# A branch for each weight tile instead of each pair of tiles, in a mixture-of-experts stage on TensorE

## The chip, the cores and the metric

The kernel runs on one core of one Trainium2 chip. The metric is device time in microseconds, from launch to end, as the median of the runs shown. TensorE (PE) multiplies, VectorE (DVE) and ScalarE (ACT) work on elements, SyncE (SP) issues the loads from HBM.

## The reference, cut to what matters

A two-layer backbone for 256 tokens of width 1024. The part that the change touches is the last one, a top-2-of-8 mixture of SwiGLU experts with an inner width of 3584, all in float32:

```python
def moe_swiglu(h, router_w, wg, wu, wd):
    logits = (h @ router_w).astype(jnp.float32)
    top_v, top_i = lax.top_k(logits, TOP_K)
    gates = jax.nn.softmax(top_v, axis=-1)
    dense_gate = jnp.sum(jax.nn.one_hot(top_i, N_EXPERTS, dtype=jnp.float32)
                         * gates[..., None], axis=-2).astype(h.dtype)
    out = jnp.zeros_like(h)
    for e in range(N_EXPERTS):
        out = out + dense_gate[..., e:e + 1] * swiglu(h, wg[e], wu[e], wd[e])
    return out
```

where `swiglu(h, wg, wu, wd)` is `(silu(h @ wg) * (h @ wu)) @ wd`.

## The kernel before, in words

Each expert's tokens are gathered by a product with a one-hot matrix (`Expert.gather`, L1103) into at most 128 columns, and after the expert scattered back in the same manner (`scatter`, L1178). The expert's weights come in tiles of 128 x 2048 float32, 1 MB each, in the order in which they are used (`Weights`, L908): 336 tiles for the eight experts, 42 for one expert. A tile is loaded by SP into one of six raw buffers (L934), then split into two float32r parts: ACT casts it to the high part `mh` (L948), and DVE subtracts that from the tile for the low part `ml` (L949). Either part has five buffers, so a split can run at most some tiles ahead of the products that read it.

The inner width is cut into seven chunks of 512 (`NCH`). A chunk has two tiles of the gate matrix (group G), two of the up matrix (group U) and, one chunk later, two of the down matrix (group D). G and U go into a PSUM bank each, are copied by ACT (`copied`, L1136), turned by PE (`turn`, L1141: transposes, or products with `fold`), go through the SiLU on ACT and the product on DVE (`act`, L1150, tile `m_sg`), and are split again into `moe_aT`, the stationary operand of D.

An expert with fewer than 65 tokens is **light**: its activations' high and low parts stand side by side in one stationary operand of 128 columns, so that two products for each weight slice (L1078, L1079) do what takes three (L142 to L144) in a **full** expert. Which it is, is known only at run time, so PE holds both versions and chooses with a branch (`arms`, L1189, branch at L1194). Expert 0 has no branch (`lights[0]` is None) and is always full.

`group` (L1213) writes out one group of two tiles. Before its products it has the splits of two later tiles written out, and between these two the work that was kept in `late`: what follows the group before (copies, SiLU, `moe_aT`, the gating of an expert's result) and the gathers and scatters that `after` has put on a later step. Then come the two tiles' products inside one branch. With `tiles.stop` the first tile behind the group, the lines are

```python
for n in range(tiles.stop + 1, tiles.stop + 4):
    W.split(n)
    W.load(n + 6)
    if n == tiles.stop + 2:
        while late:
            late.pop(0)()
parts = [W.parts.pop(n) for n in tiles]
arms(light, lambda arm: body(parts, arm))
```

A split with argument n has all tiles below n split. In the order of the source, a group's products therefore stand behind the splits of three tiles beyond the group. The order in which ACT, DVE and SP finally work is not this one: the framework's scheduler places each instruction by its own account of when it could run. A branch's two bodies are one unit to it, into which nothing else is put; what belongs to other engines lies in the stretch between two branches.

Of the kernel before, what the change touches and what calls it, by code (L numbers as in the profile page):

```python
# [18 lines left out]
P = 128  # L19
D = 1024  # L20
KT = D // P
# [7 lines left out]
D_FE = 3584  # L29
# [45 lines left out]
def hybrid_kernel(  # L75
# [26 lines left out]
    def bank(name, pool=None):  # L102
        pool = pool or psa
        return pool.tile([P, 512], F32, tag="bank", name=name)
# [518 lines left out]
    for s, (k0, k1) in enumerate(STAGES):  # L623
# [8 lines left out]
        w = split(qk, f"qk{k0}")  # L632
        modulated(hT, rx, m_x, hm, k0, k1, "xx")

        def products(rows, which, f0):
            for i in which:
                for k in range(k0, k1):
                    rows.one(i, k, *(p(k - k0)[:, f0:f0 + 512] for p in w))
                if k1 == KT:
                    rows.done(i, rows.pss[i])  # L640
# [267 lines left out]
    class Weights:  # L908
# [17 lines left out]
        @staticmethod  # L926
        def down(e, ci):
            return [(moe_w_down[e, 2 * ci + b], 2) for b in range(2)]
# [24 lines left out]
    W = Weights()  # L953
# [96 lines left out]
    def pick(w, e, *at):  # L1050
        return w[(e, *at)] if isinstance(e, int) else w[(bass.ds(e, 1), *at)].rearrange("o p f -> (o p) f")
# [31 lines left out]
    def whole(src, k, name):  # L1083
        return split(load(src, k, name), name, True)

    class Expert:
# [40 lines left out]
            self.ohT = sp.tile([P, S], F32R, tag="ohT", name=self.n + "_ohT")  # L1127
            A.copy(self.ohT, self.po[:, :S])

        def up(self, o, parts, light):  # L1130
            for half in range(2):
                for j in range(4):
                    k = 4 * half + j
                    products(o, self.xg, k, tuple(w[:, j, :] for w in parts[half]), light, k == 0, k == KT - 1)

        def copied(self, o, name):  # L1136
            c = x2k(name)
# [3 lines left out]
        def turn(self, pts, gu, light):  # L1141
            for pt, src in zip(pts, gu):
                for i in range(4):
                    o = pt[:, i * P:(i + 1) * P]
                    if light:
                        T.matmul(o, src[:, i * P:(i + 1) * P], fold, start=True, stop=True)
                    else:
                        T.transpose(o, src[:, i * P:(i + 1) * P], ident)
# [5 lines left out]
            self.aT = in_pairs(at[:, 1024 * (ci % 2):1024 * (ci % 2) + 1024], 4)  # L1154
            split_pairs(self.aT, sg)

        def down(self, ci, parts, light):
            aT = self.aT
            for b in range(2):
                k0 = ci * 4 + 2 * b  # L1160
                last = k0 + 2 == D_FE // P
                for j, i in [(j, i) for i in range(2) for j in range(2)] if last else [(j, i) for j in range(2) for i in range(2)]:
                    o = slice(i * 512, (i + 1) * 512)
                    products(self.y[i], aT, 2 * b + j, tuple(w[:, j, o] for w in parts[b]), light, k0 + j == 0, k0 + j == D_FE // P - 1)

        def down_half(self, i, parts, light):

            for k in range(4):
                products(self.y[i], self.aT, k, tuple(w[:, k, :] for w in parts[0]), light, False, k == 3)

        def gated(self, i):
            src = x2k(f"{self.n}_yg{i}")
# [16 lines left out]
    def arms(light, body):  # L1189

        if light is None:
            body(False)
        else:
            with tc.If(light > 0) as narrow:  # L1194
                body(True)
            with narrow.Else():
                body(False)

    ex = Expert(0, posm, 0, "m0")
# [5 lines left out]
    lights = [None] * NE  # L1205
# [5 lines left out]
    late = []  # L1211

    def group(light, body, then=lambda: None):  # L1213

        nonlocal step
        tiles = W.groups[step]
        for n in range(tiles.stop + 1, tiles.stop + 4):
            W.split(n)
            W.load(n + 6)
            if n == tiles.stop + 2:  # L1220
                while late:
                    late.pop(0)()
        parts = [W.parts.pop(n) for n in tiles]
        arms(light, lambda arm: body(parts, arm))
        late.append(then)
        late.extend(todo_after.pop(step, ()))
        step += 1

    def turned(x, ci, gu):
        pts = [bank(f"{x.n}_{ci}_t{m}", psb) for m in range(2)]  # L1230
        return pts, (lambda arm: x.turn(pts, gu, arm)), (lambda: x.act(ci, pts))
# [3 lines left out]
    for e in range(NE):  # L1235
        light = lights[e]
        for ci in range(NCH):
            gu = []
            _, turn, acted = turned(ex, ci - 1, prev[2]) if ci else nothing
            if ci:  # L1240
                behind.clear()
            o = bank(f"{ex.n}_{ci}_0")
            places = ci == 0
            if places:
                ex.po = bank(ex.n + "_ohp", psb)

            def gates_up(parts, arm, o=o):
                turn(arm)
                if places:
                    ex.places(arm)  # L1250
                ex.up(o, parts, arm)

            def gates_then(o=o, ex=ex, ci=ci, gu=gu, acted=acted, places=places):
                if places:
                    ex.placed()
                acted()
                gu.append(ex.copied(o, f"{ex.n}_{ci}_g"))

            group(light, gates_up, gates_then)
            u = bank(f"{ex.n}_{ci}_1")  # L1260
            group(light, lambda parts, arm: ex.up(u, parts, arm), lambda u=u, x=ex, ci=ci, gu=gu: gu.append(x.copied(u, f"{x.n}_{ci}_u")))
            if (e, ci) == (0, 1):
                over = gates()
                flush()
            if prev is not None:
                px, pi, _ = prev
                if pi == 0:
                    px.y = [bank(f"{px.n}_y{i}", psc) for i in range(2)]
                if ci == NCH - 1:
                    _, turn, acted = turned(ex, ci, gu)  # L1270
                else:
                    turn, acted = nothing[1:]

                def downs(parts, arm):
                    px.down(pi, parts, arm)
                    turn(arm)

                def downs_then(acted=acted, px=px, pi=pi):
                    acted()
                    if pi == NCH - 1:  # L1280
                        ys = [px.gated(i) for i in range(2)]
                        for i in range(2):
                            for t in range(NT):
                                after(1 + 2 * i + t, lambda x=px, t=t, i=i: x.scatter(t, i, ys[i], first=x.e == 0))

                group(lights[px.e], downs, downs_then)
            if ci == NCH - 3 and e + 1 < NE:
                nxt = Expert(e + 1, posm, (e + 1) % 2, f"m{e + 1}")
                nxt.positions()
                for b in range(2):  # L1290
                    after(b, lambda b=b, x=nxt: x.gather(b))
            prev = (ex, ci, gu)
        last = ex
        if e + 1 < NE:
            ex = nxt
            lights[e + 1] = nc.values_load(few[0:1, e + 1:e + 2], engines=(mybir.EngineType.PE,), min_val=0, max_val=1)
    for i in range(2):
        group(lights[-1], lambda parts, arm: last.down_half(i, parts, arm))
        y = last.gated(i)
        for t in range(NT):  # L1300
            last.scatter(t, i, y, pool=psb)
            store(t, i)


    with tc.If(over > 0):
        pos2 = sp.tile([P, NT, NE], F32, tag="pos2", name="pos2")
        V.tensor_scalar(pos2, posm, -float(P), None, op0=ALU.add)
        with tc.For_i(0, NE) as ev:
            ex = Expert(ev, pos2, 0, "v")
            ex.positions()  # L1310
            for b in range(2):
                ex.gather(b)
            ex.po = bank("v_ohp", psb)
            ex.places(False)
            ex.placed()
            ex.y = [bank(f"v_y{i}", psc) for i in range(2)]

            for ci in range(NCH):
                gu = []
                for m in range(2):  # L1320
                    o = bank(f"v_{ci}_{m}")
                    ex.up(o, [whole(pick((moe_w_gate, moe_w_up)[m], ev, ci, half), 4, f"v{ci}_{m}_w{half}") for half in range(2)], False)
                    gu.append(ex.copied(o, f"v_{ci}_{m}c"))
                _, turn, acted = turned(ex, ci, gu)
                turn(False)
                acted()
                ex.down(ci, [whole(pick(moe_w_down, ev, 2 * ci + b), 2, f"v{ci}d{b}") for b in range(2)], False)
            for i in range(2):
                y = ex.gated(i)
                for t in range(NT):  # L1330
                    ex.scatter(t, i, y)
        for i in range(2):
            for t in range(NT):
                store(t, i)
# [52 lines left out]
```

## Time and profile before

| | us |
|---|---|
| median of 3 runs (1473.71 to 1480.41) | 1473.93 |
| the profiled execution, its own time | 1478.5 |
| its span, from the first to the last instruction | 1476.7 |
| granted clock of TensorE over the span, 1 is full | 0.987 |

The eight experts run from about 506 us to the end; in order they are full, light, light, light, full, full, light, light, and each but the first begins at the transposes of line 1124. In a row of a timeline stand the start, the duration, the engine, the line, the operation and `out<-in`, and in brackets how long the engine stood idle before it and what ended that. A matmul's duration is longer than its share of the engine, since matmuls overlap: the step from one start to the next is what it costs.

### The profile page before, as it was taken

The numbers are of one execution on the slowest core, as the hardware profiler recorded it, in microseconds if no ns is written. First come the engines' busy times: TensorE is split into PE (matmuls) and PEld (weight loads), VectorE is DVE, ScalarE is ACT, GpSimd is POOL, SyncE is SP. The second block draws the span as 40 slices with busy tenths as digits, with TensorE's granted clock in tenths as the row PEclk, the third lists the DMA queues.
The fourth block names the chain that finished last, engine by engine and source line by source line (L and its number), as shares of the span: only waits on it lengthen the run. The fifth ranks groups of instructions, "written<-read, shape, count | busy, mean of one in ns | idle before, by whom it ended". The sixth has DMA issues, their size and how long they took to land.

```text
span 1476.7 us, 19854 instructions
## 1 busy us (share of the span) xinstructions
PE 1390.9 (94%) x7746; PEld 1151.7 (78%) x7746; DVE 1226.8 (83%) x1256; ACT 974.0 (66%) x891; POOL 1.9 (0%) x7
## 2 busy tenths in 40 slices
PE   6999999999999999999989989999999999899897
PEld 4667789999979888877767767777888888677675
DVE  4687588776666698899999998998888879899897
ACT  3444354433354576788887887886777768788785
POOL 0000000000000000000000000000000000000000
PEclk9999999999999999999999999999999999999999
DMA  9554488776654698899998998998978988899894
GB/s 367 226 219 166 155 335 323 286 274 251 245 224 176 240 402 330 326 340 395 403 398 343 408 398 334 416 385 338 365 294 331 365 343 349 331 421 386 336 413 189
DMA packets 66784, 473.53 MB, mean 321 GB/s; under 512 B 7376, under 2 KB 7760, under 8 KB 9696
## 3 DMA queue, kind: packets, MB, share of 16 engines
q1 hardware_dynamic: 66464, 471.16, 82.0%
q8 instruction: 93, 1.52, 0.4%
q0 software_dynamic: 192, 0.56, 0.2%
q14 instruction: 35, 0.29, 0.1%
HBM read 470.64 MB, written 1.05 MB: 319 GB/s over the span
## 4 chain that ended last, share of the span: by engine, by line
PE 59%; DVE 20%; issue 9%; ACT 8%; DMA 5%; DVEq 0%; SPq 0%; ACTq 0%
DVE ml L949 13%; ACT mh L948 5%; PE m L142 5%; PE m L144 5%; PE m L143 5%; PE fg_ps L164 4%; PE fd L164 4%; PE fu_ps L164 4%; PE m_y L144 2%; PE m_y L142 2%; PE m_y L143 2%; PE so_ps L164 2%; PE ada L259 2%; PE su_ps L164 2%; DMA mw<-in_moe_w_gate_dram 1%
## 5 line engine op out<-in xcount | busy, mean ns | idle before, releaser
L949 DVE TENSOR_TENSOR ml<-mw,mh 128x2048 fp32r<-128x2048 f32 x336 | 757.1, 2286 | 47.9 <-ACT mh L948 44.9
L948 ACT CAST mh<-mw 128x2048 fp32r<-128x2048 f32 x336 | 631.2, 1910 | 12.4 <-PE so_ps L164 4.1
L1079 PE MATMUL m<-ml,m_xg 128*128 128x512 f32 x560 | 223.3, 399 | 5.7 <-DVE ml L949 5.7
L1078 PE MATMUL m<-mh,m_xg 128*128 128x512 f32 x560 | 224.1, 400 | 0.0
L1078 PE MATMUL m_y<-mh,moe_aT 128*128 128x512 f32 x280 | 118.2, 422 | 25.3 <-DVE moe_aT L218 21.4
L142 PE MATMUL m<-mh,m_xg 128*128 128x512 f32 x336 | 134.5, 401 | 0.6 <-ACT m_xg L217 0.6
L1079 PE MATMUL m_y<-ml,moe_aT 128*128 128x512 f32 x280 | 121.3, 433 | 13.8 <-DVE ml L949 11.9
L1079 PEld LDWEIGHTS m<-ml,m_xg 128*128 128x128 f32 x560 | 105.2, 188 | 37.0 <-DVE ml L949 14.6
L144 PE MATMUL m<-mh,m_xg 128*128 128x512 f32 x336 | 132.9, 396 | 0.0
L143 PE MATMUL m<-ml,m_xg 128*128 128x512 f32 x336 | 132.7, 395 | 0.0
L1078 PEld LDWEIGHTS m<-mh,m_xg 128*128 128x128 f32 x560 | 105.3, 188 | 22.6
L1079 PEld LDWEIGHTS m_y<-ml,moe_aT 128*128 128x128 f32 x280 | 56.4, 201 | 45.3 <-DVE ml L949 34.3
L1078 PEld LDWEIGHTS m_y<-mh,moe_aT 128*128 128x128 f32 x280 | 56.7, 203 | 41.3 <-ACT mh L948 19.3
L217 ACT CAST moe_aT<-m_sg 128x512 fp32r<-128x512 f32 x56 | 37.4, 669 | 72.5 <-DVE m_sg L1153 72.5
L142 PEld LDWEIGHTS m<-mh,m_xg 128*128 128x128 f32 x336 | 65.6, 195 | 13.3 <-ACT m_xg L217 1.5
L144 PEld LDWEIGHTS m<-mh,m_xg 128*128 128x128 f32 x336 | 65.5, 195 | 12.5
L143 PEld LDWEIGHTS m<-ml,m_xg 128*128 128x128 f32 x336 | 65.7, 196 | 11.9
L1152 ACT ACTIVATE m_sg<-m_t 128x512 f32<-128x512 f32 x56 | 33.6, 599 | 53.5 <-PE m L142 26.7
L144 PE MATMUL m_y<-mh,moe_aT 128*128 128x512 f32 x168 | 66.4, 396 | 0.7 <-DVE moe_aT L218 0.7
L143 PE MATMUL m_y<-ml,moe_aT 128*128 128x512 f32 x168 | 66.4, 395 | 0.0
L142 PE MATMUL m_y<-mh,moe_aT 128*128 128x512 f32 x168 | 66.2, 396 | 0.0
L164 PE MATMUL fd<-a,fd_hi 128*128 128x256 f32 x352 | 63.0, 281 | 0.0
(410 smaller groups left out, 2663.8 us busy)
## 6 DMA issues: line engine op xcount, KB each, us to landing
mw<-in_moe_w_gate_dram SPq DMA_DIRECT2D x112, 1024.0 KB, 7.1
mw<-in_moe_w_up_dram SPq DMA_DIRECT2D x112, 1024.0 KB, 7.1
mw<-in_moe_w_down_dram SPq DMA_DIRECT2D x110, 1024.0 KB, 6.8
ada<-in_ada_w_dram SPq DMA_DIRECT2D x40, 1024.0 KB, 4.9
fg_w<-in_ffn_w_gate_dram SPq DMA_DIRECT2D x11, 1024.0 KB, 5.2
fu_w<-in_ffn_w_up_dram SPq DMA_DIRECT2D x11, 1024.0 KB, 5.4
fd<-in_ffn_w_down_dram SPq DMA_DIRECT2D x11, 1024.0 KB, 5.0
adap<-in_ada_pairs_dram SPq DMA_DIRECT2D x8, 1024.0 KB, 9.6
```

The source lines that it names most:

```text
L142: T.matmul(o, lh, rh, start=start, stop=False)
L143: T.matmul(o, lh, rl, start=False, stop=False)
L144: T.matmul(o, ll, rh, start=False, stop=stop)
L164: self.newest = m = T.matmul(o, lhsT, rhs, start=self.first is None, stop=stop, skip_group_check=True)
L217: A.copy(hi, src)
L259: queued(T.matmul(pa[32 * j:32 * j + 32, :r.shape[2]], stat[:, 4 * half + j, :], r[:, j, :], start=(first and half == 0), stop=(last and h ...
L948: queued(A.copy(hi, r), "A")
L949: queued(V.tensor_tensor(lo, r, hi.bitcast(F32), op=ALU.subtract), "V")
L1078: T.matmul(o, x, wh, start=start, stop=False)
L1079: T.matmul(o, x, wl, start=False, stop=stop)
L1152: A.activation(sg, pts[0], AF.Silu)
```

## The change

The branch is made for each tile: `up` and `down` take one tile (a half, or b) instead of both, and `group` goes through its tiles one by one. Before each tile's products it has the splits written out up to four tiles beyond that tile, then whatever is in `late`. The turn stands in the first tile's branch of G, or, at an expert's last chunk, in the second tile's branch of D. The overflow path (`tc.If(over > 0)`), which is not run here, is rewritten to the new arguments.

```diff
-        def up(self, o, parts, light):
-            for half in range(2):
-                for j in range(4):
-                    k = 4 * half + j
-                    products(o, self.xg, k, tuple(w[:, j, :] for w in parts[half]), light, k == 0, k == KT - 1)
+        def up(self, o, half, parts, light):
+            for j in range(4):
+                k = 4 * half + j
+                products(o, self.xg, k, tuple(w[:, j, :] for w in parts), light, k == 0, k == KT - 1)
...
-        def down(self, ci, parts, light):
-            aT = self.aT
-            for b in range(2):
-                k0 = ci * 4 + 2 * b
...
+        def down(self, ci, b, parts, light):
+            k0 = ci * 4 + 2 * b
...
     def group(light, body, then=lambda: None):
...
-        for n in range(tiles.stop + 1, tiles.stop + 4):
-            W.split(n)
-            W.load(n + 6)
-            if n == tiles.stop + 2:
-                while late:
-                    late.pop(0)()
-        parts = [W.parts.pop(n) for n in tiles]
-        arms(light, lambda arm: body(parts, arm))
+        for i, n in enumerate(tiles):
+            W.split(n + 5)
+            W.load(n + 11)
+            while late:
+                late.pop(0)()
+            parts = W.parts.pop(n)
+            arms(light, lambda arm: body(i, parts, arm))
...
-            def gates_up(parts, arm, o=o):
-                turn(arm)
-                if places:
-                    ex.places(arm)
-                ex.up(o, parts, arm)
+            def gates_up(half, parts, arm, o=o):
+                if half == 0:
+                    turn(arm)
+                    if places:
+                        ex.places(arm)
+                ex.up(o, half, parts, arm)
...
-                def downs(parts, arm):
-                    px.down(pi, parts, arm)
-                    turn(arm)
+                def downs(b, parts, arm):
+                    px.down(pi, b, parts, arm)
+                    if b:
+                        turn(arm)
```

## Rows read from the trace of the kernel before

**Rows 1.** The page: span, and busy time of each engine.
```profile
span 1476.7 us, 19854 instructions
PE 1390.9 (94%) x7746; PEld 1151.7 (78%) x7746; DVE 1226.8 (83%) x1256; ACT 974.0 (66%) x891; POOL 1.9 (0%) x7
```

**Rows 2.** Busy time by stretch: experts 1, 3, 5, 6, 7, then one light chunk.
```profile
core 0: us, PE busy (x) PEld busy (x) DVE busy (x) ACT busy (x) POOL busy (x), PEclk, DMA share, GB/s
629.45:741.45 112.00, 102.94 (x499) 81.26 (x499) 107.90 (x76) 95.26 (x80) 0.00 (x0) 1.00 0.97 381
...
857.36:973.35 115.99, 104.42 (x490) 81.50 (x490) 110.16 (x77) 95.02 (x80) 0.00 (x0) 0.97 0.95 382
...
1103.25:1234.20 130.95, 129.86 (x602) 109.40 (x602) 111.21 (x77) 95.83 (x80) 0.00 (x0) 1.00 0.89 337
1234.20:1349.19 114.99, 104.94 (x498) 83.22 (x498) 109.47 (x76) 95.03 (x80) 0.00 (x0) 0.97 0.96 382
1349.19:1470.25 121.06, 107.37 (x482) 82.08 (x482) 112.73 (x74) 92.54 (x75) 0.00 (x0) 0.97 0.84 335
...
792.48:806.89 14.41, 13.65 (x66) 10.56 (x65) 14.41 (x9) 13.04 (x11) 0.00 (x0) 1.00 0.99 389
```

**Rows 3.** Timeline of DVE in a light expert's steady chunks.
```profile
800.61 11.10 DVE L949 TENSOR_TENSOR ml<-mw,mh 128x2048 fp32r<-128x2048 f32 x5
811.62 0.68 DVE L1153 TENSOR_TENSOR m_sg<-m_t,m_sg 128x512 f32<-128x512 f32 x1
...
814.42 0.69 DVE L218 TENSOR_TENSOR moe_aT<-m_sg,moe_aT 128x512 fp32r<-128x512 f32 x1
```

**Rows 4.** Timeline of PE and ACT there: the turn, the SiLU, U to D.
```profile
807.78 1.06 PE L1146 MATMUL m_t<-fold,m_u 128*128 128x128 f32 x8
808.45 0.59 ACT L1152 ACTIVATE m_sg<-m_t 128x512 f32<-128x512 f32 x1
...
816.06 0.40 PE L1079 MATMUL m<-ml,m_xg 128*128 128x512 f32 x1
...
816.29 0.40 PE L1078 MATMUL m_y<-mh,moe_aT 128*128 128x512 f32 x1
```

**Rows 5.** Line 1194, the branches: count, shortest/median/longest in ns, first and last.
```profile
L1194 PEldq COMPARE_BRANCH  x254: 65/174/352, 628.1 to 1463.0; - x127
```

**Rows 6.** Timeline of ACT in a full expert: the SiLU behind a turn.
```profile
1012.16 0.60 ACT L1152 ACTIVATE m_sg<-m_t 128x512 f32<-128x512 f32 x1 [3.75 <-PE m L142]
```

**Rows 7.** Timeline of PE around the scatter of expert 1, inside expert 2.
```profile
764.65 0.39 PE L1182 MATMUL m_sc<-m_ylo,m_ohT 128*128 128x512 f32 x1
769.64 0.76 PE L1078 MATMUL m_y<-mh,moe_aT 128*128 128x512 f32 x1 [4.59 <-DVE moe_aT L218]
...
776.12 0.40 PE L1182 MATMUL m_sc<-m_yhi,m_ohT 128*128 128x512 f32 x1
```

**Rows 8.** Timeline of DVE in the same stretch.
```profile
766.00 0.69 DVE L1153 TENSOR_TENSOR m_sg<-m_t,m_sg 128x512 f32<-128x512 f32 x1
...
768.80 0.69 DVE L218 TENSOR_TENSOR moe_aT<-m_sg,moe_aT 128x512 fp32r<-128x512 f32 x1
...
770.06 2.29 DVE L949 TENSOR_TENSOR ml<-mw,mh 128x2048 fp32r<-128x2048 f32 x1
776.78 0.75 DVE L1184 SCALAR_TENSOR_TENSOR moe_acc<-m_sc,gate,moe_acc 128x512 f32<-128x512 f32 x1 [4.43 <-PE m_sc L1182]
```

**Rows 9.** Busy time by stretch: D of that chunk (columns as in rows 2).
```profile
770.00:776.20 6.20, 6.20 (x17) 4.80 (x17) 2.35 (x2) 5.05 (x3) 0.00 (x0) 0.55 0.98 371
```

**Rows 10.** Waits of DVE: experts 1 to 3, then 6 and 7 (total, times, longest).
```profile
DVE moe_acc L1184 <- PE m_sc L1182: 9.7, 3, 4.5
...
DVE moe_acc L1184 <- PE m_sc L1182: 8.5, 2, 4.3
```

**Rows 11.** Waits of DVE in the full experts 4 and 5 (same columns).
```profile
DVE m_sg L1153 <- PE m L143: 7.1, 6, 1.5
```

More of the change, by code (lines that the diff above doesn't have):

```diff
@@ L1155, in act @@
             split_pairs(self.aT, sg)
-        def down(self, ci, parts, light):
-            aT = self.aT
-            for b in range(2):
-                k0 = ci * 4 + 2 * b
[L1161 to L1164, printed above, removed]
+        def down(self, ci, b, parts, light):
+            k0 = ci * 4 + 2 * b
+            last = k0 + 2 == D_FE // P
+            for j, i in [(j, i) for i in range(2) for j in range(2)] if last else [(j, i) for j in range(2) for i in range(2)]:
+                o = slice(i * 512, (i + 1) * 512)
+                products(self.y[i], self.aT, 2 * b + j, tuple(w[:, j, o] for w in parts), light, k0 + j == 0, k0 + j == D_FE // P - 1)
         def down_half(self, i, parts, light):
             for k in range(4):
-                products(self.y[i], self.aT, k, tuple(w[:, k, :] for w in parts[0]), light, False, k == 3)
+                products(self.y[i], self.aT, k, tuple(w[:, k, :] for w in parts), light, False, k == 3)
         def gated(self, i):
@@ L1260, in hybrid_kernel @@
             u = bank(f"{ex.n}_{ci}_1")
-            group(light, lambda parts, arm: ex.up(u, parts, arm), lambda u=u, x=ex, ci=ci, gu=gu: gu.append(x.copied(u, f"{x.n}_{ci}_u")))
+            group(light, lambda half, parts, arm: ex.up(u, half, parts, arm), lambda u=u, x=ex, ci=ci, gu=gu: gu.append(x.copied(u, f"{x.n}_{ci}_u")))
             if (e, ci) == (0, 1):
@@ L1297, in hybrid_kernel @@
     for i in range(2):
-        group(lights[-1], lambda parts, arm: last.down_half(i, parts, arm))
+        group(lights[-1], lambda _, parts, arm: last.down_half(i, parts, arm))
         y = last.gated(i)
@@ L1321, in hybrid_kernel @@
                     o = bank(f"v_{ci}_{m}")
-                    ex.up(o, [whole(pick((moe_w_gate, moe_w_up)[m], ev, ci, half), 4, f"v{ci}_{m}_w{half}") for half in range(2)], False)
+                    for half in range(2):
+                        ex.up(o, half, whole(pick((moe_w_gate, moe_w_up)[m], ev, ci, half), 4, f"v{ci}_{m}_w{half}"), False)
                     gu.append(ex.copied(o, f"v_{ci}_{m}c"))
@@ L1326, in hybrid_kernel @@
                 acted()
-                ex.down(ci, [whole(pick(moe_w_down, ev, 2 * ci + b), 2, f"v{ci}d{b}") for b in range(2)], False)
+                for b in range(2):
+                    ex.down(ci, b, whole(pick(moe_w_down, ev, 2 * ci + b), 2, f"v{ci}d{b}"), False)
             for i in range(2):
```

## The prediction

> **What bounds the kernel now.** I read the page first. It has PE busy for 94% of the span and DVE for 83% [rows 1], which would point at PE; but both are averages over experts with different limits, so the next view is busy time by stretch, one stretch an expert [rows 2]. There the reader sees two kinds. In a full expert PE is busy 129.86 of 130.95 us: it is the bound, and only 1.1 us of it is idle. In a light expert (857.36 to 973.35) PE is busy 104.42 of 115.99 us, but DVE 110.16. In a light chunk away from the expert's edges DVE is busy for all of its 14.41 us.
>
> The timeline of DVE says why [rows 3]: five splits in a row take 11.10 us, so from start to start one takes (11.10 - 2.28)/4 = 2.21 us. Six splits for a chunk are 13.2 us, and m_sg and moe_aT take some 0.6 us each: 14.4 us, the length of the chunk. PE needs less: 48 products at 0.23 us a step [rows 4] are 11.0 us, plus about 1.8 us for a turn. So **light experts are bound by DVE, full ones by PE**, and a wait is worth something only where it stops the binding engine. That leaves 1.1 us in a full expert. In the light ones it leaves DVE's idle time: 112.00 - 107.90 = 4.1 in expert 1, 115.99 - 110.16 = 5.8 in expert 3 and as much in expert 2, 114.99 - 109.47 = 5.5 in expert 6, 121.06 - 112.73 = 8.3 in expert 7, whose stretch has the tail [rows 2]: 29.5 us together. This is the most that any better order of these queues can bring.
>
> Most of it is one wait. DVE waits for the scatter (line 1184 for line 1182) 9.7 us in experts 1 to 3 and 8.5 us in experts 6 and 7 [rows 10]; four of these five waits are about 4.4 us, one in each of experts 2, 3, 6 and 7, 9.7 + 8.5 - 0.8 = 17.4 us. The first of them stands in [rows 7 to 9]: DVE reaches m_sg only at 766.00 and moe_aT at 768.80, behind splits and the gating of the expert before. PE, done with U's products and a scatter at 765.04, stands idle for 4.59 us until moe_aT is there. [...] The scatter is queued behind D on PE, and moe_acc waits for the scatter on DVE, in front of the next splits: 4.43 us in which the binding engine does nothing.
>
> **The change, part by part.** *Branches.* By the code 146 groups with a branch have two tiles and two have one, so 148 branches become 294. A light arm leaves two records (the compare and the jump past the other arm), a full arm one: 148 + 106 = 254 today [rows 5], 294 + 210 = 504 after, 250 more. At the median of 174 ns they cost 43 us if each stopped PE. They do not stop it today: at the change from U to D, across a branch, the step is 816.29 - 816.06 = 0.23 us, the same as within a group [rows 4]. The sequencer is ahead by the products queued behind the last wait. With half as long an arm there are still 8 products, 8 x 0.23 = 1.8 us, to hide two records of at most 0.35 us each. I take nothing; the bounds are 0 and +43, the first being the nearer, since the row is of this very branch.
>
> *Releases.* In a full expert the SiLU waits until PE is already in the products at line 142 [rows 6], since one count has to serve two arms of different length. An arm of one tile differs by 4 products instead of 8, so this release, and that of the split buffers, comes up to 4 x 0.23 = 0.9 us sooner. It lands on ACT and DVE in experts where PE binds: nothing, between 0 and -1.1 us an expert (PE's idle time), 3 us for the three full ones. In light experts nothing, as the SiLU starts there at 808.45, before its turn ends at 808.84 [rows 4].
>
> *Splits and loads.* The number of splits, loads, products and bytes is unchanged. In the source the split of the fourth tile ahead now precedes what is in late, and the next split stands between the two tiles' products. SP's loads wait for raw buffers that a split frees, so they follow DVE. A light expert's 42 tiles, 44.0 MB, come at 382 GB/s in 116 us [rows 2]; without any wait of DVE they would have to come in 110 us, at 400 GB/s. The chunk from 792.48 has 389 at a share of 0.99 [rows 2], so DMA is close behind; I allow it to give back 3 us in all, between 0 and the whole gain.
>
> *Order on DVE.* Here the time lies, and the trace before cannot show the new queue; it must be bounded. A group's products are now two units for the scheduler instead of one. What depends on the first (the turn, and behind it SiLU, m_sg and moe_aT) no longer has to follow both tiles' splits, and can be placed one split, 2.2 us, earlier. At the scatter this has a clear worth: moe_aT at 766.6 instead of 768.8, PE idle for 2.4 us instead of 4.59, D over 767.4 to 771.1 at full clock, the scatter done at 771.8, while DVE is at its split until 770.06 + 2.29 = 772.35. DVE then finds the scatter done and the 4.43 us vanish. Four times: 17.4 us. The bounds are 0 (the order stays) and -29.5 (all of DVE's idle time goes); above zero it is the rival below. I take the 17.4, nearest to the rows, less the 3 for DMA.
>
> **Sum.** 0 + 0 - 17.4 + 3 = -14 us. The profiled execution took 1478.5 us, of which 1476.7 is the span; it lies 4.6 above the median of 1473.93, inside the runs shown. So 1478.5 becomes 1464, and the median 1460. A measurement of this kernel can tell about 0.5%, 7.4 us, from no change.
>
> [...]
>
> **The rivals.** *Nothing moves.* DVE binds the light experts and PE the full ones, and no part of the change takes an instruction from either. If the scheduler goes on placing m_sg and moe_aT behind two splits, the four waits stay, and the time is 1474, within 5 us. For it: the splits were never a shortage that a deeper order could fill, as DVE has nothing to spare. Against: the stretches between branches, by which the order is made, all change.
>
> *DVE meets PE too early (slower).* In DVE's queue m_sg stands two splits or more behind the turn: the turn ends at 808.84 and m_sg starts at 811.62 [rows 3, 4]. One split earlier, 809.4, it is just ready (the SiLU ends at 809.04). Two splits earlier, 807.2, it would wait 1.8 us in each light chunk, with the next split queued behind it on the binding engine. The point from which it decides is thus between one and two splits. The nearest row for its price is the same wait where it exists today, in full experts: 7.1 us in 6 times, 1.2 us each [rows 11]. In 30 light chunks (five experts, six away from the edge) 1.2 us are 35 us; less the 17.4 that the scatter gives back, +18: 1492. If all the 1.8 us are paid, 54 - 17 = +37, 1511.
>
> *Branches come onto the path (slower).* If PE stops for half of the 250 new records, 125 x 0.174 = 22 us, 1496, or 1482 with the gain. Against it is the step across the branch.
>
> **How the numbers follow.** The forecast (the scatter's waits go, for the most part) has 0.47, nothing moves 0.31, DVE meeting PE too early 0.17, exposed branches 0.05. Faster by over 0.5%: nearly all of the forecast's cases, 0.45. Slower by over 0.5%: the last two, 0.22. The same: 0.33. The range leaves out 2 in 10: below, the gain beyond 24 us of the 29.5 (1450); above, the worse half of the slower cases, beyond 1492. The forecast's own range is 1450 to 1466.
>
> **What would show it.** Right: in experts 2, 3, 6 and 7 no wait of moe_acc above 2 us, no stretch with a clock below 1 there, DVE still fully busy in a light chunk of 14.4 us, 504 branch records and 0.23 us steps across them; a light expert near 111 to 112 us, a full one still at 130 to 131. Wrong: the 4.4 us waits still there (then nothing moved); DVE's m_sg waiting for the turn or the SiLU in each light chunk, which would be longer than 14.4 us; PE steps above 0.3 us at tile borders with no wait named, the branches' share. A light chunk shorter than 14.4 us would refute the bound itself.

## The result, and the profile after

The changed kernel takes 1491.07 us (median of 4 runs, 1490.01 to 1492.56) against 1476.11 for the kernel before beside it: a ratio of 1.0101, with a 95% interval of 1.0085 to 1.0118. It is **slower by 1.0%**, where the forecast was 1460 and faster.

The page and then the view of busy time by stretch, for experts 1, 3, 5 and 7 (to the end of the span) and for one steady light chunk, answer to [rows 1, 2]; the columns are those of [rows 2].

```profile
span 1488.2 us, 20100 instructions
PE 1396.1 (94%) x7746; PEld 1146.3 (77%) x7746; DVE 1226.9 (82%) x1256; ACT 976.4 (66%) x891; POOL 1.9 (0%) x7
```

```profile
625.22:743.48 118.26, 106.26 (x499) 82.77 (x499) 108.02 (x76) 95.61 (x79) 0.00 (x0) 0.97 0.93 364
860.44:977.45 117.01, 104.53 (x490) 79.97 (x490) 110.17 (x77) 95.51 (x79) 0.00 (x0) 0.99 0.96 379
1110.80:1244.98 134.18, 131.53 (x603) 110.59 (x603) 111.08 (x77) 95.96 (x79) 0.00 (x0) 0.99 0.88 329
1361.93:1488.20 126.27, 108.03 (x482) 80.67 (x482) 113.94 (x75) 93.00 (x75) 0.00 (x0) 0.97 0.82 328
789.92:804.73 14.81, 14.00 (x65) 10.49 (x64) 14.49 (x9) 13.04 (x10) 0.00 (x0) 1.00 1.01 414
```

DVE does the same work as before: 1226.9 us in all, 110.17 in expert 3. So the length of a light expert is still that work plus DVE's idle time, and only the idle time has changed: in expert 3 from 5.8 to 6.8 us, in expert 1 from 4.1 to 10.2. The full expert 5 went from 130.95 to 134.18. Only the stretch from expert 7 to the end of the span became shorter, from 127.51 to 126.27 us; expert 7 has no next expert to gather for. The seven stretches sum to 15.7 us more than before: 10.3 of it in the light experts 1, 2, 3 and 6, and 6.7 in the full experts 4 and 5. There PE is the bound, and in expert 5 it is busy for 131.53 us instead of 129.86 and idle for 2.7 instead of 1.1. (The profiled execution came to expert 1 4.2 us earlier than before's, in stages that the change does not touch, so the spans differ by 11.5.)

**What went away.** The view of waits of DVE in experts 1 to 3 (total, times, longest) has one row left, so the 9.7 us of moe_acc in [rows 10] are gone. Behind it stands the only row that moe_acc has in the whole kernel, all of it in the full experts 4 and 5:

```profile
DVE ml L949 <- ACT mh L948: 23.8, 14, 6.0
```

```profile
DVE moe_acc L1181 <- PE m_sc L1179: 2.1, 4, 1.1
```

The timelines of PE and DVE at the place that answers to [rows 7], one expert later, show why: D's first product now waits 1.60 us for moe_aT instead of 4.59, the products behind it step by 0.23 us (888.63 - 888.40 for the last one), and the scatter is done just before DVE asks for it.

```profile
886.70 0.47 PE L1078 MATMUL m_y<-mh,moe_aT 128*128 128x512 f32 x1 [1.60 <-DVE moe_aT L218]
...
888.40 0.39 PE L1079 MATMUL m_y<-ml,moe_aT 128*128 128x512 f32 x1
888.63 0.40 PE L1179 MATMUL m_sc<-m_yhi,m_ohT 128*128 128x512 f32 x1
...
889.10 0.39 PE L1078 MATMUL m_y<-mh,moe_aT 128*128 128x512 f32 x1
...
885.86 0.69 DVE L218 TENSOR_TENSOR moe_aT<-m_sg,moe_aT 128x512 fp32r<-128x512 f32 x1
...
889.32 0.74 DVE L1181 SCALAR_TENSOR_TENSOR moe_acc<-m_sc,gate,moe_acc 128x512 f32<-128x512 f32 x1
```

Two things have moved here. DVE has seven splits instead of eight between the m_sg of the chunk before and this one (20.11 us from one m_sg to the other, 22.05 before), so moe_aT and what follows it on DVE come one split earlier. And the scatter, which stood behind all 16 products of D, now stands behind the first eight, in the gap between D's two branches; D goes on at 889.10. Behind all of D it would be done some 1.9 us later (an estimate, 8 x 0.23 us), and DVE would wait for about as long.

**What came.** DVE's remaining row is the new loss: `ml` waits for the cast `mh`, at most 6.0 us. The timeline shows it near the end of an expert, where the next expert's tokens are gathered. Here are PE, ACT and DVE in expert 3:

```profile
951.81 0.49 PE L1109 MATMUL m_pg<-m_oh,h 128*128 128x128 f32 x2 [1.27 <-DVE m_t L1118]
953.98 1.28 PE L1109 MATMUL m_pg<-m_oh,h 128*128 128x128 f32 x10
958.75 0.61 PE L1109 MATMUL m_pg<-m_oh,h 128*128 128x128 f32 x4
962.74 0.50 PE L1078 MATMUL m<-mh,m_xg 128*128 128x512 f32 x1 [1.51 <-ACT mh L948]
965.07 0.80 PE L1079 MATMUL m<-ml,m_xg 128*128 128x512 f32 x1 [1.82 <-DVE ml L949]
...
952.36 1.90 ACT L948 CAST mh<-mw 128x2048 fp32r<-128x2048 f32 x1
959.39 1.51 ACT L1116 ACTIVATE m_t<-m_pg,modT,a_m 128x128 f32<-128x128 f32 x4 [5.14 <-PE m_pg L1109]
960.78 1.91 ACT L948 CAST mh<-mw 128x2048 fp32r<-128x2048 f32 x1
...
962.72 2.29 DVE L949 TENSOR_TENSOR ml<-mw,mh 128x2048 fp32r<-128x2048 f32 x1 [5.96 <-ACT mh L948]
```

The gather's 16 products are in no branch. Before, the second gather stood in one piece; these are PE and ACT of the kernel before at the same place, and then ACT's waits of m_t in the whole kernel (total, times, longest), before and after:

```profile
953.32 1.95 PE L1109 MATMUL m_pg<-m_oh,h 128*128 128x128 f32 x16
...
955.31 1.50 ACT L1116 ACTIVATE m_t<-m_pg,modT,a_m 128x128 f32<-128x128 f32 x4 [0.32 <-PE m_pg L1109]
```

```profile
ACT m_t L1116 <- PE m_pg L1109: 11.0, 7, 4.4
```

```profile
ACT m_t L1116 <- PE m_pg L1109: 34.1, 7, 6.3
```

After, the second gather's products are spread over the more numerous stretches between branches, as 2, 10 and 4. The last four stand behind a turn and the first tile of G, and end at 959.36. ACT's four m_t wait for them 5.14 us, with the next casts queued behind; DVE runs out of casts and stops for 5.96 us; then PE, 1.51 and 1.82 us, and its granted clock falls to 0.60 on average from 965.5 to 969.0. In full experts, where PE binds, PE itself stops for 0.59 + 1.82 us there.

ACT waits here for all of the gather's products. By 955.3 twelve of them, three of the four parts that m_t reads, were done, and ACT still started m_t only at 959.39, behind the last four. Why the first three parts did not start earlier is not shown. The cast behind m_t starts at 960.78, as the four end (959.39 + 1.51 = 960.90).

A second, smaller loss lies in the steady light chunk, 14.81 us instead of 14.41. ACT's and DVE's timelines in such a chunk:

```profile
805.82 0.60 ACT L1151 ACTIVATE m_sg<-m_t 128x512 f32<-128x512 f32 x1 [1.10 <-PE m_t L1145]
...
796.25 11.20 DVE L949 TENSOR_TENSOR ml<-mw,mh 128x2048 fp32r<-128x2048 f32 x5
807.37 0.69 DVE L1152 TENSOR_TENSOR m_sg<-m_t,m_sg 128x512 f32<-128x512 f32 x1
808.25 2.29 DVE L949 TENSOR_TENSOR ml<-mw,mh 128x2048 fp32r<-128x2048 f32 x1 [0.20 <-ACT mh L948]
```

The SiLU stands one cast earlier in ACT's queue, meets a turn that has not ended, and holds the next cast for 1.10 us. DVE pays 0.20 us at that cast here (0.30 in the chunk before), and its five splits in a row take 11.20 us instead of the 11.10 of [rows 3].

**Branches.** Line 1191 answers to [rows 5]:

```profile
L1191 PEldq COMPARE_BRANCH  x504: 65/176/396, 623.9 to 1472.9; - x168
```

There are twice as many, as counted, and the products do not show it. Where PE changes from U to D the records run ahead of the products. In before, at the change of [rows 4], the two start at 814.6 and 814.9, behind U's last wait (for ml, until 814.56), and D's first product starts only at 816.29. After, at the change ahead of the SiLU shown above, they start at 798.6 and 798.8, behind a wait for ml until 798.59, and D's first product starts at 800.32, 0.22 us behind the start of U's last. This is the view of busy time for 11.70 us from just behind the start of the full expert 4, and below it the same stretch of before, with the same 52 products:

```profile
977.60:989.30 11.70, 11.70 (x52) 9.83 (x52) 10.34 (x7) 7.13 (x7) 0.00 (x0) 1.00 0.99 383
```

```profile
973.50:985.20 11.70, 11.70 (x52) 9.82 (x52) 11.46 (x8) 8.73 (x8) 0.00 (x0) 1.00 0.98 387
```

### The profile page after: what moved, and what is told of

Read it like the earlier page. It is cut to its first block, busy times and chain, and to the rows that moved or that the text cites. A ratio compares the mean times of both kernels' runs of the same rounds, so it can differ in the third digit from the quotient of the medians.

```text
span 1488.2 us, 20100 instructions
## 1 busy us (share of the span) xinstructions
PE 1396.1 (94%) x7746; PEld 1146.3 (77%) x7746; DVE 1226.9 (82%) x1256; ACT 976.4 (66%) x891; POOL 1.9 (0%) x7
## 4 chain that ended last, share of the span: by engine, by line
PE 61%; DVE 22%; issue 10%; ACT 6%; DMA 1%; SPq 0%; DVEq 0%; ACTq 0%
DVE ml L949 15%; PE m L143 5%; PE m L144 5%; PE m L142 5%; ACT mh L948 5%; PE fg_ps L164 4%; PE fd L164 4%; PE fu_ps L164 4%; PE m_y L144 2%; PE m_y L142 2%; PE m_y L143 2%; PE m L1079 2%; PE so_ps L164 2%; PE ada L259 2%; PE m_y L1079 2%
## 5 line engine op out<-in xcount | busy, mean ns | idle before, releaser
L1079 PE MATMUL m<-ml,m_xg 128*128 128x512 f32 x560 | 230.5, 412 | 23.7 <-DVE ml L949 23.4
L1078 PE MATMUL m<-mh,m_xg 128*128 128x512 f32 x560 | 228.9, 409 | 7.0 <-ACT mh L948 6.1
L1079 PEld LDWEIGHTS m<-ml,m_xg 128*128 128x128 f32 x560 | 107.5, 192 | 67.0 <-DVE ml L949 45.6
L142 PE MATMUL m<-mh,m_xg 128*128 128x512 f32 x336 | 136.4, 406 | 1.8 <-ACT mh L948 1.2
L143 PE MATMUL m<-ml,m_xg 128*128 128x512 f32 x336 | 134.4, 400 | 3.6 <-DVE ml L949 3.6
L144 PE MATMUL m<-mh,m_xg 128*128 128x512 f32 x336 | 134.2, 399 | 0.0
L1078 PEld LDWEIGHTS m<-mh,m_xg 128*128 128x128 f32 x560 | 107.8, 193 | 30.4 <-ACT mh L948 7.8
L1079 PE MATMUL m_y<-ml,moe_aT 128*128 128x512 f32 x280 | 116.7, 417 | 7.6 <-DVE ml L949 5.3
L1078 PE MATMUL m_y<-mh,moe_aT 128*128 128x512 f32 x280 | 112.7, 402 | 10.9 <-DVE moe_aT L218 10.9
L1079 PEld LDWEIGHTS m_y<-ml,moe_aT 128*128 128x128 f32 x280 | 53.1, 190 | 39.1 <-DVE ml L949 29.3
L143 PEld LDWEIGHTS m<-ml,m_xg 128*128 128x128 f32 x336 | 66.5, 198 | 16.4 <-DVE ml L949 4.5
L142 PEld LDWEIGHTS m<-mh,m_xg 128*128 128x128 f32 x336 | 66.4, 198 | 15.4 <-ACT mh L948 2.0
L144 PEld LDWEIGHTS m<-mh,m_xg 128*128 128x128 f32 x336 | 66.2, 197 | 12.8
L1078 PEld LDWEIGHTS m_y<-mh,moe_aT 128*128 128x128 f32 x280 | 53.2, 190 | 23.0 <-ACT mh L948 10.0
L142 PE MATMUL m_y<-mh,moe_aT 128*128 128x512 f32 x168 | 66.5, 398 | 0.0
L143 PE MATMUL m_y<-ml,moe_aT 128*128 128x512 f32 x168 | 66.4, 395 | 0.0
L144 PE MATMUL m_y<-mh,moe_aT 128*128 128x512 f32 x168 | 66.2, 395 | 0.0
L1137 ACT COPY m_u<-m 128x512 f32<-128x512 f32 x56 | 32.8, 587 | 46.3 <-PE m L144 34.5
```

The costliest lines, as they stand in the source:

```text
L142: T.matmul(o, lh, rh, start=start, stop=False)
L143: T.matmul(o, lh, rl, start=False, stop=False)
L144: T.matmul(o, ll, rh, start=False, stop=stop)
L1078: T.matmul(o, x, wh, start=start, stop=False)
L1079: T.matmul(o, x, wl, start=False, stop=stop)
L1137: A.copy(c, o)
```

## Experiments

Expectations that speak of "after" mean the changed kernel. Every kernel computes the whole result.

### Which part of the change it is

Two kernels take the change apart. The first keeps the branch for each tile and goes back to the old order of splits in the source; the second does the reverse.

```diff
 # tile_branch_old_splits, in group()
-        for i, n in enumerate(tiles):
-            W.split(n + 5)
-            W.load(n + 11)
-            while late:
-                late.pop(0)()
+        for n in range(tiles.stop + 1, tiles.stop + 4):
+            W.split(n)
+            W.load(n + 6)
+            if n == tiles.stop + 2:
+                while late:
+                    late.pop(0)()
+        for i, n in enumerate(tiles):
             parts = W.parts.pop(n)
             arms(light, lambda arm: body(i, parts, arm))
 # pair_branch_new_splits, in group()
         for i, n in enumerate(tiles):
             W.split(n + 5)
             W.load(n + 11)
-            while late:
-                late.pop(0)()
-            parts = W.parts.pop(n)
-            arms(light, lambda arm: body(i, parts, arm))
+            if i == 0:
+                while late:
+                    late.pop(0)()
+                pair = [W.parts.pop(m) for m in tiles]
+                arms(light, lambda arm: [body(j, p, arm) for j, p in enumerate(pair)])
```

> The changed kernel with its branch for each tile, but the splits, the loads and what is in late written out in the order of the kernel before. Theory (the number of branches alone does it: two units for the scheduler instead of one decide what it puts between them, and the order in the source decides nothing): 1491 us, within 4, as the changed kernel, with the same two new waits (ACT's m_t for the gather near 34 us in all, DVE's ml for ACT's mh in each light chunk). Rival (the order of splits and late in the source does it): back to 1476 us, with the 4.4 us waits of moe_acc for the scatter back in experts 2, 3, 6 and 7.

> The other half: one branch for each pair of tiles as before, but late written out behind the split of the fourth tile ahead, and the next split behind the products. Theory (the branches alone): 1476 us, within 4, with the scatter waits of 4.4 us, light chunks of 14.4 us and ACT's m_t waiting for the gather some 11 us in all as before. Rival (source order): 1491 us, light chunks of 14.8 us.

Measured: 1491.38 us, ratio 1.0108 (1.0094 to 1.0123), and 1473.83 us, ratio 0.9995 (0.9985 to 1.0004). Expert 3 of the two kernels, by the view of busy time:

```profile
863.92:980.88 116.96, 104.62 (x490) 79.78 (x491) 110.14 (x77) 95.51 (x79) 0.00 (x0) 0.99 0.95 377
```

```profile
854.90:970.90 116.00, 104.20 (x490) 81.58 (x490) 110.34 (x77) 95.39 (x80) 0.00 (x0) 0.97 0.96 381
```

The branch alone makes the whole difference: 116.96 us, against 117.01 after. The order of splits in the source does nothing: 116.00 us, against 115.99 before.

### The gather in one piece

The gather's products move into the branch of a following tile, as one run that nothing can part.

```diff
+            first = inside.pop(step, None) if i == 0 else None
...
+                b, x = first
+                pg = bank(f"{x.n}_pg{b}", psd)
+
+                def both(arm):
+                    x.gather_mm(b, pg)
+                    body(i, parts, arm)
+
+                arms(light, both)
+                late.append(finish.pop(step))
...
-                    after(b, lambda b=b, x=nxt: x.gather(b))
+                    inside[step + b + 1] = (b, nxt)
+                    finish[step + b + 1] = lambda b=b, x=nxt: x.gather_fin(b)
```

> The changed kernel, but the 16 products of a gather's half stand in front of a tile's products inside that tile's branch, so that no branch of another tile can come between them. Theory (the largest part of the loss is ACT waiting for the last gather products, which stand behind a turn and a tile on PE, with the next casts queued behind that wait): the waits of DVE of 6 us in experts 1, 2, 3 and 6 go, and the 2.4 us of PE in experts 4 and 5: 4 x 6 + 2 x 3.3 = 31 us less, 1460 us, within 6; a light expert falls from 117 to 111. Rival (the casts and splits would be held up elsewhere, DMA or the scatter's order giving the loss anyway): within 8 us of 1491.

Measured: 1476.53 us, ratio 1.0007 (0.9996 to 1.0018): 14.5 us less than after, half of what was expected. Experts 2 and 3 by the view of busy time, and PE's timeline at the second gather of expert 3:

```profile
742.53:858.25 115.72, 104.64 (x491) 81.76 (x491) 110.42 (x77) 95.61 (x79) 0.00 (x0) 0.97 0.97 382
858.25:972.56 114.31, 103.21 (x490) 80.58 (x491) 110.33 (x77) 95.45 (x79) 0.00 (x0) 0.99 0.98 387
```

```profile
949.63 3.40 PE L1112 MATMUL m_pg<-m_oh,h 128*128 128x128 f32 x16 [3.87 <-DVE m_t L1124]
```

The wait of 5.96 us is gone, but both gathers use the one bank of `psd`, and PE is now ready for the second (945.76) 5.7 us after it began the first (940.08); before, 16 us lay between the two. The second must wait until DVE has read the first with its four m_t, which stand between splits. PE stops for 3.87 us, and the casts on ACT are late again behind m_t and m_xg: DVE still idles for 4.0 us in expert 3 and 5.3 in expert 2.

### The SiLU behind one more cast

A dependence without a semaphore puts the SiLU behind the cast of the third tile from the group's first.

```diff
-            A.activation(sg, pts[0], AF.Silu)
+            m = A.activation(sg, pts[0], AF.Silu)
+            if behind is not None:
+                tc.add_manual_dep(m.ins, W.casts[behind].name, mybir.DependencyInfo(
+                    mybir.DependencyClass.NoSync, mybir.DependencyReason.DATA), reason="the cast first")
...
-                acted()
+                acted(g0 + 2)
```

> The changed kernel, but ACT's SiLU of a chunk may be placed only behind the cast of the second tile after the turn's tile, where it stood before. Theory (in each light chunk ACT waits about 1.1 us for the turn with the next cast behind it, and DVE then 0.4 us for that cast): light chunks fall from 14.8 to 14.4 us, about 25 of them, 10 us less, 1481 us, within 4; the gather's waits stay. Rival (the chunk is longer because PE stops at twice as many branches): light chunks stay at 14.8 us and the time at 1491.

Measured: 1487.48 us, ratio 1.0083 (1.0070 to 1.0096). DVE's timeline from one steady chunk to the next:

```profile
912.89 0.68 DVE L1156 TENSOR_TENSOR m_sg<-m_t,m_sg 128x512 f32<-128x512 f32 x1
...
927.30 0.68 DVE L1156 TENSOR_TENSOR m_sg<-m_t,m_sg 128x512 f32<-128x512 f32 x1
```

The chunk is 927.30 - 912.89 = 14.41 us again, without a wait. The cause is right, and its size was overrated: 3.6 us in all. By the views of busy time 0.8 to 0.9 us go in each of experts 1, 3, 4 and 6 (expert 3 from 117.01 to 116.21) and 1.2 from expert 7 to the end. Of the six steps from one m_sg to the next in expert 3, three change, from 45.3 to 44.5 us together; the others hold the scatter or the gather. Expert 4 is a full one, and why it gains is not shown.

### The branch for each tile at the scatter alone

If the gain and the losses lie in different places, the branch can be made for a tile only where it gains.

```diff
-    def group(light, body, then=lambda: None):
+    def group(light, body, then=lambda: None, single=False):
...
+            if single:
+                parts = W.parts.pop(n)
+                arms(light, lambda arm: body(i, parts, arm))
+            elif i == 0:
+                pair = [W.parts.pop(m) for m in tiles]
+                arms(light, lambda arm: [body(j, p, arm) for j, p in enumerate(pair)])
...
-            group(light, gates_up, gates_then)
+            group(light, gates_up, gates_then, ci == 1)
```

(and likewise for the groups U and D)

> A branch per tile in the three groups of an expert's second chunk alone, where the scatter of the expert before stands; a branch per pair everywhere else. If the change's gain (scatter) and its losses (gather, SiLU) are separate in place, this keeps the gain alone: the four long waits of moe_acc go (4.5 us in the second expert after a light one, four times), the gather's products stand in one piece again and the steady light chunk is 14.4 us, so 1475 - 17 = 1458 +- 4. Rival: with moe_acc gone, the casts or PE stop DVE for as long at the same place, and the time stays at 1471 to 1478. Second rival: the smaller units upset the gather even from that distance, 1480 and more.

Measured: 1471.44 us, ratio 0.9976 (0.9965 to 0.9988), so most of the gain did not come. DVE's timeline at the scatter in expert 3, then experts 3 and 4 by the view of busy time:

```profile
884.15 0.75 DVE L1181 SCALAR_TENSOR_TENSOR moe_acc<-m_sc,gate,moe_acc 128x512 f32<-128x512 f32 x1 [1.93 <-PE m_sc L1179]
```

```profile
851.41:964.85 113.44, 103.24 (x490) 81.25 (x491) 110.33 (x77) 95.16 (x80) 0.00 (x0) 0.97 0.98 391
964.85:1097.18 132.33, 129.63 (x595) 108.79 (x595) 112.09 (x78) 96.22 (x80) 0.00 (x0) 0.99 0.89 335
```

With the chunk ahead still in pairs, moe_aT comes as late as before (PE waits 4.60 us for it at 879.51), and only the second half of the gain is there: the scatter no longer stands behind all of D but behind its first tile, and the wait is 1.93 us instead of 4.4. The full experts 4 and 5 lose 2.4 and 3.0 us (129.90 and 130.95 before); why is not shown. By this the other half of the gain comes from the smaller units ahead of the scatter; they were not tried alone.

### Both losses taken out, and the gathers apart

The next two kernels have the gather in the branch and the SiLU behind the cast; the second also puts the second gather three groups behind the first instead of one.

```diff
-                    inside[step + b + 1] = (b, nxt)
-                    finish[step + b + 1] = lambda b=b, x=nxt: x.gather_fin(b)
+                    inside[step + 1 + 3 * b] = (b, nxt)
+                    finish[step + 1 + 3 * b] = lambda b=b, x=nxt: x.gather_fin(b)
```

> After, with the gather's 16 products inside a tile's branch and the SiLU behind the cast of the third tile. Theory (the two costs are separate): 1476.5 - 3.6 = 1473 +- 3, the light chunk at 14.41 us. Rival: in the stretch with the gather the wait moves from the SiLU to the gather's PSUM bank, and nothing is gained on the kernel with the gather alone: 1476 to 1478.

> As the kernel with both edits, but the second gather's products stand three groups behind the first's instead of one. Theory: what was left of the gather's cost is PE's wait of 3.87 us for the one PSUM bank that both gathers use (m_pg on m_t of DVE) and the 1.4 to 1.9 us waits of DVE for casts that follow it; about 3 us in each of four or five light experts, so 1473 - 13 = 1460 +- 5. Rival: ACT's four m_t then stand beside the next SiLU and stop the casts there as they did in after: 1472 to 1480.

Measured: 1471.71 us, ratio 0.9973 (0.9960 to 0.9986), and **1458.95 us, ratio 0.9890 (0.9869 to 0.9912)**, faster than both kernels. In the first PE waits 3.87 us for m_t at the second gather as it did with the gather alone, and DVE idles 4.5 us in expert 3. In the second, the view of waits of DVE in expert 3 has one row, and the view of busy time shows experts 3 and 5 so:

```profile
DVE ml L950 <- ACT mh L949: 1.4, 3, 0.9
```

```profile
849.42:960.94 111.52, 101.85 (x491) 79.11 (x491) 110.09 (x77) 95.09 (x79) 0.00 (x0) 1.00 0.99 394
1089.71:1219.38 129.67, 129.42 (x602) 109.48 (x602) 110.77 (x77) 96.37 (x79) 0.00 (x0) 1.00 0.90 341
```

DVE is busy for 110.09 of 111.52 us in the light expert, PE for 129.42 of 129.67 in the full one: the two bounds that the prediction named, with next to nothing left to win by order in these two experts.

### Does the gain come from the branch or from the gather's place?

A control has the branch per pair with these gathers; the other kernel has the branch per tile with these gathers and without the edit to the SiLU.

```diff
 # pair_gather_apart3, in group()
+                def both(arm):
+                    if first:
+                        first[1].gather_mm(first[0], pg)
+                    for j, p in enumerate(pair):
+                        body(j, p, arm)
+
+                arms(light, both)
```

> The control of the fastest kernel so far: the branch per pair as before, with the gather's products inside a pair's branch and the two gathers three groups apart. Theory: the 16 us that the per-tile kernel with these gathers won over before come from the scatter's waits, which only the per-tile branch removes; here moe_acc's wait of 4.5 us in each light expert stays and only before's 1.1 us wait near the gather can go, so 1475 - 4 = 1471 +- 4. Rival: the gather's new place alone brings the gain, with whichever branch: 1459 +- 4.

> The fastest kernel so far without the order set for the SiLU. Theory: each steady light chunk is 14.8 us again instead of 14.4, worth the 3.6 to 4.8 us that the same edit was worth on the two other kernels: 1459 + 4 = 1463 +- 3. Rival: with the gather out of the way the casts stand far enough ahead to hide the SiLU's wait, 1458 to 1460.

Measured: 1476.96 us, ratio 1.0007 (0.9998 to 1.0016), and 1461.69 us, ratio 0.9897 (0.9882 to 0.9912). The waits of DVE on the scatter in the whole kernel, in the control and then with the branch per tile:

```profile
DVE moe_acc L1187 <- PE m_sc L1185: 19.8, 9, 3.3
```

```profile
DVE moe_acc L1187 <- PE m_sc L1185: 2.1, 4, 1.1
```

The gathers' new place brings nothing by itself. It is no neutral control, though: the long waits of moe_acc fall from 4.5 to 3.3 us, and PE gets a new wait for ACT's SiLU at an expert's first transposes, 16.8 us in all (1.8 before). With the same gathers, the branch per tile takes 15.3 us off (1476.96 - 1461.69). By the views of busy time 10.7 us of this lie in the light experts and 4.0 in the full experts 4 and 5; of the 17.7 us of moe_acc's waits that go with it, 12.6 stood in the light ones. The SiLU's edit is worth 2.7 us here by the medians, or 1.9 by each kernel's distance from the kernel before beside it.

## Why the prediction was wrong

- **What bounds the kernel**: right. DVE's busy time is the same in all of them (1226.8 us before, 1226.9 after, 1225.2 in the fastest), the time followed DVE's idle time in light experts and PE's time in full ones, and the best kernel stopped at 111.5 and 129.7 us, near where the text had put the bounds.
- **Branches at nothing**: right. 504 records, no step across them; the fastest kernel has all of them. The longest record went from 352 to 396 ns, and the products step as before: 0.22 us from U to D, and the same 52 products in 11.70 us.
- **Releases at nothing**: after, the change cost the full experts 6.7 us. With the gathers mended they take 128.78 and 129.67 us, 1.1 and 1.3 us less than before, about the bound that the text gave for each. The release does come sooner, by 0.95 us where the text had up to 0.9: in the chunk of [rows 6] the SiLU was released by the fourth product behind the turn and started 1.23 us behind the first (1012.16 - 1010.93); after, in the same chunk of expert 4, the turn itself releases it, and it starts 0.28 us behind the first product (1014.20 - 1013.92). The SiLU's wait for the products at line 142, 26.7 us in eight times before, has no row in the kernel with the gathers mended; whether earlier releases are the reason was not tried apart.
- **Splits and loads, +3**: the order of the splits in the source does nothing (the second experiment). The loads gave nothing back either: in the fastest kernel they run at 394 GB/s in expert 3, where [rows 2] have 382, and ACT waited for a load once, for 0.6 us. They do follow DVE: SP waits for DVE's ml 772.2 us in 309 times before, and 765.0 in 302 after. The term was about 0.
- **Order on DVE, -17.4**: this is the step that failed, by what it left out. Its own part came true in the main. The four long waits are gone, moe_aT comes one split earlier, PE is idle there for 1.60 us instead of 4.59, and over D the granted clock is 1.00 in all four experts: in expert 3, D's products start from 886.70 to 890.97, 4.27 us with a scatter between them, where before's D of [rows 7] took 6.48 us (769.64 to 776.12) at 0.55. But the last link of the chain was wrong. The text moved moe_aT up by a split and left DVE's asking for the scatter at 772.35, 5.75 us behind it; in the trace everything behind moe_aT on DVE moved with it, and DVE asks 3.46 us behind moe_aT (889.32 - 885.86). The scatter is in time because, by the estimate above, it moved up between D's two tiles, which the text did not foresee; the kernel with the branch per tile at the scatter alone has that move without an earlier moe_aT, and its wait is 1.93 us instead of 4.5. With the gathers mended the light experts are together 12.0 us shorter than before by the views of busy time, or 14.8 with the SiLU mended too, where the text had 17.4.
- **Where it failed**: the step was looked at for DVE only. It said that what depends on a group's first tile can stand one split earlier, and costed that on DVE's queue at the scatter. Two more things move when the units get smaller, both met on ACT, whose queue the text never costed in light experts, so the sum has no term for them. The gather's products lie between branches too, and were spread over more gaps, so that ACT's m_t met PE; and the SiLU moved ahead of one cast and met the turn. ACT itself is never the bound (busy for 95.51 of 117.01 us in expert 3, after), but its casts feed DVE, which is.
- **The sizes**: after is 15.0 us above the before beside it, and the kernel with the gathers mended 14.0 below its own, so the gather as the change left it cost 29 us. The SiLU's edit took 3.6, 4.8 and 2.7 us off the three kernels on which it was tried, by medians of runs taken at different times, between which before itself moved by up to 1.3 us. That the kernel with the gathers mended lands on the -14 of the sum is luck: the light experts gave 12.0 instead of 17.4, the full ones 2.4 instead of nothing, and the loads took nothing back.
- **The rivals**: "DVE meets PE too early" gave the right direction and, by luck, nearly the time (1492), since its path is another: m_sg of a light chunk does not wait for the turn; ACT does, for 1.10 us in the chunk shown, and at the gather for 5.14. The price of 1.2 us in each of 30 chunks is refuted: a steady chunk lost 0.4 us. "Nothing moves" and "exposed branches" are refuted.
- **What would show it**: the conditions on moe_acc, the clock at the scatter, the branch records and the steps came true; the light chunk of 14.4 us, the light expert of 111 to 112 and the full one of 130 to 131 did not, and that is where the loss was found.

Three things stay open. Why the scheduler parts the gather's products when the units are smaller is not shown, only that it does so whatever the order of the splits. A second PSUM bank for the gather, which might take the 3.87 us wait away in another manner than by distance, was not tried. How much of the full experts' 2.4 us comes from earlier releases is not known.

## What to carry to other kernels

When a unit that a scheduler cannot enter is made smaller, everything that lies outside such units can be placed anew, not only what the edit aims at: list those instructions (here scatter, gather, turn's consumers) and ask of each what stands behind it in its queue. A queue that is far from full can still be the one that matters, if it feeds the engine that bounds the stage; here a wait of 5.1 us on ACT, 66% busy, cost DVE 6.0 us. And before an edit is given up for its sum, take its trace apart by place: this one held a gain of some 16 us and losses of some 31, and the losses could be undone by themselves.

## What was not expected of the hardware

Some stops of PE cost more than their own length. After two stops of 1.51 and 1.82 us with one product between them the granted clock of the next 3.5 us was 0.60, and the products from 965.66 to 968.22 stepped by 0.43 us instead of 0.23:

```profile
965.50:969.00 3.50, 3.50 (x10) 2.53 (x10) 3.50 (x5) 2.77 (x4) 0.00 (x0) 0.60 0.72 279
```

After the stop of 3.87 us the 16 products of a gather took 3.40 us instead of 1.95. After a single stop of 1.60 us the products went on at 0.23 us a step, at a granted clock of 1.00.
